# Loading the first four row tiles of x already cast, from GpSimd's queue

## The chip, the cores and the metric

The kernel runs on one core of one Trainium2 chip. A core has a matrix engine (TensorE, PE in the profile; PEld is its loading of weights), a vector engine (VectorE, DVE), an engine for activations and copies (ScalarE, ACT), GpSimd (POOL) and SyncE (SP), which here does nothing but issue transfers. Data move between the chip's memory and the core's on-chip memory (SBUF) by 16 DMA engines. The engines run on their own and wait for one another by semaphores; each works through its instructions in the order in which the program has them. The metric is the device time of one execution in microseconds (us), lower is better.

## What is computed

```python
def setup_inputs():
    B, S, D = 8, 2048, 2048
    # x: [B, S, D] float32, w: [D, D] float32, both normally distributed

def reference(x, w):
    cs = np.cumsum(x, axis=1)
    diff = cs - np.concatenate([zeros, cs[:, :-1, :]], axis=1)
    return np.matmul(diff, w).astype(np.float32)
```

The difference of a running sum is the sequence itself, so the output is x times w up to rounding: 16384 rows of x, in 128 row tiles of 128 rows, by a matrix of 2048 x 2048. The kernel computes that product and no running sum.

## The kernel before, in words

The 128 row tiles are worked in two ways. The first four (`PLAIN = 4`) are multiplied plainly in bf16, while w is still coming in. All others go in groups of four through a scheme of seven products for each two-by-two split, in f16, with scaled blocks of w that stay in SBUF; 31 such groups fill the time from about 70 us to the end. Which instruction comes when on each engine is written out by hand: every operation is recorded with a label (`record`), the table `places` gives each label a number for its period, and `emit` sorts by that number. So the numbers set only the order on each engine; the data dependences set the waits.

The opening stage is the one that the change touches (period 0 of `places`).

- w is loaded in 32 chunks of 512 KB (`fetch`, L281): label `w.h.ko` is rows 128 ko to 128 ko + 127, half h of the columns. Each chunk lands as f32 in its own place, `rest(h, ko)`. ScalarE then casts it to bf16 into a ring of seven buffers (`taken`, L287), and VectorE takes the largest magnitude of each row of it (L291), from which the scale of the f16 blocks comes (L402 to L409).
- x of the first four tiles is loaded in 16 pieces of 256 KB (`load_x`, L245): label `first x.q.r` is row tile r, columns 512 q to 512 q + 511. The pieces lie as f32 in places of w's second half that are not loaded yet (`resting(KH - 1 - q, a)`, which is the place of w.1.(7-q) or w.1.(15-q)). VectorE casts two row tiles at once to bf16 (`cast_x`, L251; label `cast x.q.a`, a = 0 for row tiles 0 and 1, a = 1 for 2 and 3) into `resting(q, 0)`, which is the place of w.1.q.
- TensorE transposes the eight 128 x 128 blocks of such a piece (`turn_x`, L260, label `turn x.q.a`) by an identity matrix, `eye`. VectorE (for q = 0) or ScalarE copies the result from PSUM into `xP` (`turned`, L270).
- The plain products are then `plain.h.r.ko` (L302): row tile r, chunk w.h.ko, two matmuls of 512 columns (one for row tile 3 with h = 0, whose other half is done late, `left over`, L430).
- The identity is made on VectorE: ones, a running count, its transpose, and four comparisons of 32 rows each (`eye_rows`, L220). In the order before, the first comparison stands early, and the other three behind the maximum of w.0.0.
- 22 matmuls on zeros (`warm.i`, L338) stand on TensorE before and between the first real ones.

All loads before the change, of x and of w, and all stores go out on SP's queue, in the order of `places`: first x.0.2, first x.0.3, w.0.0, first x.0.1, first x.0.0, w.0.3, and so on, the last piece of x (first x.3.2) between w.0.9 and w.0.11. GpSimd has nothing to do in this stage before the maximum over all partitions (L406). w.1.q can be loaded only when the transposes of x.q have read their place.

The order of TensorE in the opening: the first 15 warm matmuls, turn x.0.1, five warm ones, turn x.0.0, one warm, plain.0.2.0, one warm, plain.0.2.3, turn x.1.0, plain.0.2.1, plain.0.0.0, plain.0.0.3, plain.0.0.1, and on. Behind the plain stage follow the scaled blocks of w (L415, L417), the first tiles of the second kind (weighed at L138, scaled at L170, transposed by DMA at L187) and their products (L532, L554).

Of the kernel before, what the change touches and what calls it, by code (L numbers as in the profile page):

```python
# [10 lines left out]
def kernel(  # L11
# [6 lines left out]
    nc = tc.nc  # L18
    P = 128
# [39 lines left out]
        [p[:, i // 2, i % 2] for p in pieces] for i in range(8)  # L59
    )  # L60
    fours = Wall.bitcast(f16).rearrange("p k (i n j c) -> p k i j n c", i=4, j=2, c=NB)
    tiny = const.tile([P, 64], f32, name="tiny")
    sums_at = [tiny[:, ds(2 * i, 2)] for i in range(4)]
    means_at = [tiny[:, ds(i, 1)] for i in (8, 9, 13, 14)]
    uw, uinv, wred = (tiny[:, ds(10 + i, 1)] for i in range(3))
# [48 lines left out]
    def record(label, engine, ask):  # L114
        at = seen[period[0], label] = seen.get((period[0], label), 0) + 1
        if at > 1:
            label = f"{label}#{at}"
        ops.append((period[0], label, engine, ask))
# [90 lines left out]
    def resting(k, a):  # L209
        return whole[k][:, a, 1, :]  # L210
# [26 lines left out]
    for i in range(0, P, 32):  # L237
        eye_rows(i)

    def load_x(q, r):  # L240
        to = resting(KH - 1 - q, r // 2)[:, ds(r % 2 * NB, NB)]
        record(
            f"first x.{q}.{r}",
            "sp",
            lambda: nc.sync.dma_start(to, x2[ds(r * P, P), ds(q * KQ * P, KQ * P)]),  # L245
        )

    def cast_x(q, a):
        to = resting(q, 0).bitcast(bf16).rearrange("p (a c) -> p a c", a=2)[:, a]
        src = resting(KH - 1 - q, a)  # L250
        record(f"cast x.{q}.{a}", "dve", lambda: nc.vector.tensor_copy(to, src))  # L251
        return to

    def turn_x(q, a, src, i):
        v = banks[i].bitcast(bf16)
# [10 lines left out]
    def turned(q, a, v, engine):  # L266
        to = xP[:, ds(2 * a, 2), ds(q * KQ, KQ), :].rearrange("p r k m -> p r (k m)")
        v = v.rearrange("p (r c) -> p r c", r=2)
        on = nc.scalar.copy if engine == "act" else nc.vector.tensor_copy
        record(f"turned x.{q}.{a}", engine, lambda: on(to, v))  # L270
# [72 lines left out]
    AHEAD = 3  # L343
    done = []
    ps = [[banks[2 * r + n] for n in here(0, r)] for r in range(PLAIN)]
    loads = {2: 1, 5: 2, 9: 3}
    turns = {2: (1, 0), 3: (1, 1), 5: (2, 0), 6: (2, 1), 9: (3, 0), 10: (3, 1)}
    for ko in range(KO):
        for r in range(PLAIN):
            if ko in loads:  # L350
                load_x(loads[ko], r)
            elif ko < 2 and r // 2 == ko:
                load_x(0, r)
        fetch(0, ko)
    cast = {}
    for ko in range(KO - KQ):
        if ko == 0:
            for a in range(2):
                turned(0, a, turn_x(0, a, cast_x(0, a), 6 + a), "dve")
                if a == 0:  # L360
                    taken(0, ko)
                for r in (2 * a, 2 * a + 1):
                    plain(0, r, ko)
            continue
        if ko in turns:
            q, a = turns[ko]
            if a == 0:
                for i in range(2):
                    cast[q, i] = cast_x(q, i)
            v = turn_x(q, a, cast[q, a], 7)  # L370
            taken(0, ko)
            turned(q, a, v, "act")
        else:
            taken(0, ko)
        for r in range(PLAIN):
            plain(0, r, ko)
# [756 lines left out]
    for g in range(PLAIN + 4, END, 4):  # L1133
# [5 lines left out]

    places = {  # L1140
        0: {
            'ones': -4948, 'numbers': -4947, 'numbers turned': -4946, 'zeros': -4945,
# [524 lines left out]
```

## Time and profile before

| | us |
|---|---|
| median of 3 runs | 1461.22 |
| lowest and highest run | 1456.45, 1462.13 |
| span of the profiled execution | 1457.7 |
| TensorE busy | 1440.2 (99%) |
| VectorE busy | 1245.1 (85%) |
| ScalarE busy | 1132.1 (78%) |
| GpSimd busy | 288.1 (20%) |

The span reaches from the first to the last instruction of one execution that the hardware profiler recorded. That execution's own device time isn't listed beside it; the median of the runs lies 3.5 us above its span. The granted clock of TensorE was 0.999 over the span. A busy TensorE is not yet a TensorE at its peak, since matmuls are pipelined and their ends are modelled. In the lists of waits, a row names who waited, for whom, and for how many microseconds in total, how often, and at the longest. In the chain, a row is a piece of the path that ended last, with its start and length. Bandwidths are of the 16 DMA engines together.

### The profile page before, as it was taken

How to read it: one execution, taken by the hardware profiler on the slowest of the kernel's cores; microseconds unless marked ns; L12 is line 12 of the kernel's file. 1: busy time of each engine (PE TensorE's matmuls, PEld its weight loads, DVE VectorE, ACT ScalarE, POOL GpSimd, SP SyncE). 2: the span in 40 equal slices, each digit the busy share in tenths (PEclk: the TensorE clock that was granted, in tenths of full speed). 3: DMA queues.
4: the chain of work that ended last, by engine and by line, in shares of the span. 5: the costliest groups of instructions: out<-in, count | busy, mean ns of one | idle time of the engine just before them, and what ended most of it. 6: DMA issues, size and time to landing. Idle time of an engine off the chain costs nothing.

```text
span 1457.7 us, 20733 instructions
## 1 busy us (share of the span) xinstructions
PE 1440.2 (99%) x6692; PEld 652.4 (45%) x6698; DVE 1245.1 (85%) x2075; ACT 1132.1 (78%) x1742; POOL 288.1 (20%) x400
## 2 busy tenths in 40 slices
PE   8999999999999999999999999999999999999998
PEld 3444444444444444444444444444444444444443
DVE  6998898888888888889888889888888888898887
ACT  5886678877788877788877788877788777788773
POOL 0001122212222212222122122122122122122211
PEclk9999999999999999999999999999999999999999
DMA  9999879999888999889998889998899999889983
GB/s 354 359 255 274 220 222 250 261 263 249 252 242 241 262 266 243 239 248 243 273 269 238 236 249 240 272 258 248 223 263 247 266 253 260 224 247 260 263 212 135
DMA packets 348108, 367.33 MB, mean 252 GB/s; under 512 B 271456, under 2 KB 271456, under 8 KB 348000
## 3 DMA queue, kind: packets, MB, share of 16 engines
q1 hardware_dynamic: 348000, 366.02, 89.3%
q8 instruction: 52, 0.85, 0.2%
q14 instruction: 56, 0.46, 0.1%
HBM read 166.20 MB, written 134.74 MB: 206 GB/s over the span
## 4 chain that ended last, share of the span: by engine, by line
PE 92%; DMA 5%; ACT 1%; issue 1%; DVE 0%; SPq 0%; DVEq 0%; POOL 0%; ACTq 0%
PE b L554 60%; PE b L532 32%; DMA W<-in_w_dram 2%; DMA W<-in_x_dram 2%; DMA out_dram<-arena 0%; DMA x<-arena 0%; DMA F<-in_x_dram 0%; ACT waste L138 0%; ACT arena L287 0%; ACT F L170 0%; DVE arena L579 0%; ACT arena L318 0%; ACT arena L568 0%; ACT W L417 0%; SPq L245 0%
## 5 line engine op out<-in xcount | busy, mean ns | idle before, releaser
L532 PE MATMUL b<-W,x 128*128 128x512 f16 x2176 | 523.2, 379 | 0.6 <-DMA x<-F 0.6
L579 DVE SCALAR_TENSOR_TENSOR arena<-b,tiny,arena 128x512 f32<-128x512 f32 x612 | 439.7, 743 | 55.4 <-ACT arena L568 42.8
L554 PEld LDWEIGHTS <-arena 128*128 128x128 f16 x2700 | 264.0, 98 | 321.3 <-issue 3.5
L554 PE MATMUL b<-W,arena 128*128 128x512 f16 x1640 | 405.6, 379 | 0.6 <-ACT arena L571 0.6
L568 ACT ACTIVATE arena<-b,tiny 128x512 f32<-128x512 f32 x496 | 322.3, 685 | 51.4 <-PE b L532 39.4
L532 PEld LDWEIGHTS <-x 128*128 128x128 f16 x2176 | 212.9, 98 | 257.5 <-DMA x<-F 1.1
L170 ACT ACTIVATE F<-F,tiny 128x1024 f16<-128x1024 f32 x246 | 282.0, 1147 | 52.0 <-DVE tiny L159 47.0
L554 PE MATMUL b<-W,x 128*128 128x512 f16 x1180 | 297.1, 379 | 0.0
L571 ACT COPY arena<-b 128x512 f32<-128x512 f32 x294 | 169.7, 586 | 147.5 <-PE b L554 136.8
L138 ACT ACTIVATE waste<-F 128x1024 uint8<-128x1024 f32 x246 | 260.2, 1058 | 13.5 <-DMA F<-in_x_dram 11.7
L554 PE MATMUL b<-arena 128*128 128x512 f16 x1060 | 266.9, 379 | 0.5 <-DVE tiny L159 0.3
L520 POOL TENSOR_TENSOR arena<-x,x 128x512 f16<-128x512 f16 x118 | 142.7, 1210 | 543.9 <-PE b L554 511.9
L520 DVE TENSOR_TENSOR b<-b,arena 128x512 f32<-128x512 f32 x294 | 203.2, 692 | 38.1 <-ACT arena L571 37.3
L554 PEld LDWEIGHTS <-x 128*128 128x128 f16 x1416 | 138.5, 98 | 167.4 <-issue 0.7
L520 DVE TENSOR_TENSOR arena<-W 128x2048 f16<-128x2048 f16 (+1 forms) x127 | 149.4, 1177 | 2.8 <-PE b L554 2.5
L157 POOL TENSOR_SCALAR tiny<-tiny 128x1 f32<-128x1 f32 x124 | 41.8, 337 | 439.3 <-ACT waste L138 414.3
L571 ACT COPY b<-b 128x512 f32<-128x512 f32 x147 | 85.0, 578 | 35.8 <-DVE arena L579 20.6
L520 DVE TENSOR_TENSOR arena<-x,arena 128x512 f16<-128x512 f16 x118 | 50.2, 427 | 54.3 <-PE b L554 54.3
L520 DVE TENSOR_TENSOR x<-x,x 128x1024 f16<-128x1024 f16 x124 | 82.3, 681 | 0.2
L520 DVE TENSOR_TENSOR arena<-W,arena 128x2048 f16<-128x2048 f16 (+1 forms) x70 | 75.3, 1076 | 3.1 <-PE b L554 3.0
L160 POOL TENSOR_SCALAR tiny<-tiny 128x1 f32<-128x1 f32 x124 | 72.1, 583 | 0.7
L554 PE MATMUL b<-arena,x 128*128 128x512 f16 x236 | 60.2, 379 | 0.0
(46 smaller groups left out, 616.4 us busy)
## 6 DMA issues: line engine op xcount, KB each, us to landing
F<-in_x_dram SPq DMA_DIRECT2D x246, 512.0 KB, 5.5
out_dram<-arena SPq DMA_DIRECT2D x240, 512.0 KB, 5.4
W<-in_w_dram SPq DMA_DIRECT2D x32, 512.0 KB, 9.0
arena<-kept SPq DMA_DIRECT2D x29, 512.0 KB, 4.4
out_dram<-arena SPq DMA_DIRECT2D x32, 256.0 KB, 2.9
W<-in_x_dram SPq DMA_DIRECT2D x16, 256.0 KB, 7.6
x<-F SPq DMA_TRANSPOSE x246, 3.7
arena<-in_x_dram SPq DMA_DIRECT2D x2, 512.0 KB, 4.7
```

The costliest lines, as they stand in the source:

```text
L138: lambda: nc.scalar.activation(waste, data, ABS, scale=1.0 / ROW, accum_out=m),
L157: lambda: nc.gpsimd.tensor_scalar(m, m2[:, :1], m2[:, 1:], TINY, ADD, MAX),
L160: record(f"unit{role(t)}", "pool", lambda: nc.gpsimd.tensor_scalar(u, m, uw, None, MUL))
L170: lambda: nc.scalar.activation(to, data, COPY, scale=s),
L520: record(label, engine, lambda: on.tensor_tensor(dst, p, q, op))
L532: said = nc.tensor.matmul(to[n], a[k], b[k][:, n, :], start=(start and k == 0), stop=(k == KH - 1), skip_group_check=True,)
L554: said = nc.tensor.matmul(to, a[k], b[k], start=(start and k == 0), stop=(k == 3), skip_group_check=True)
L568: record(label, "act", lambda: nc.scalar.activation(c, p, COPY, scale=u))
L571: record(label, "act", lambda: nc.scalar.copy(to, p))
L579: label, "dve", lambda: nc.vector.scalar_tensor_tensor(c, p, u, c, MUL, ADD)
```

## The change

The sixteen f32 loads of x become eight transfers of two row tiles each, issued from GpSimd. They cast on the way, so that bf16 lands where the cast's result was put before, and the eight casts on VectorE are gone. Five of the eight stand behind a small copy on GpSimd ("seen") that reads one column of a chunk of w, and so waits until that chunk has landed; the copies' results go to a tile, `tiny`, that grows from 64 to 80 columns and are read by nobody. GpSimd's order is first x.0.1, first x.0.0, seen w.0.0, first x.1.0, first x.1.1, seen w.0.1, first x.2.0, seen w.0.6, first x.2.1, seen w.0.2, first x.3.0, seen w.0.7, first x.3.1. The four rows of the identity are made directly behind one another at the start of VectorE's order. The places of all other labels are kept.

```diff
-    tiny = const.tile([P, 64], f32, name="tiny")
+    tiny = const.tile([P, 80], f32, name="tiny")
...
-    def load_x(q, r):
-        to = resting(KH - 1 - q, r // 2)[:, ds(r % 2 * NB, NB)]
-        record(
-            f"first x.{q}.{r}",
-            "sp",
-            lambda: nc.sync.dma_start(to, x2[ds(r * P, P), ds(q * KQ * P, KQ * P)]),
-        )
-
-    def cast_x(q, a):
-        to = resting(q, 0).bitcast(bf16).rearrange("p (a c) -> p a c", a=2)[:, a]
-        src = resting(KH - 1 - q, a)
-        record(f"cast x.{q}.{a}", "dve", lambda: nc.vector.tensor_copy(to, src))
-        return to
+    def home_x(q, a):
+        return resting(q, 0).bitcast(bf16).rearrange("p (a c) -> p a c", a=2)[:, a]
+
+    def load_x(q, a, behind):
+        to = home_x(q, a).rearrange("p (r c) -> p r c", r=2)
+        src = x2[ds(2 * a * P, 2 * P), ds(q * KQ * P, KQ * P)].rearrange("(r p) c -> p r c", r=2)
+        if behind is not None:
+            seen_at = tiny[:, ds(64 + 4 * q + a, 1)]
+            first = rest(0, behind)[:, :1]
+            record(
+                f"seen.{q}.{a}", "pool", lambda: nc.gpsimd.tensor_copy(seen_at, first)
+            )
+        record(f"first x.{q}.{a}", "pool", lambda: nc.gpsimd.dma_start(to, src))
...
-    loads = {2: 1, 5: 2, 9: 3}
...
     for ko in range(KO):
-        for r in range(PLAIN):
-            if ko in loads:
-                load_x(loads[ko], r)
-            elif ko < 2 and r // 2 == ko:
-                load_x(0, r)
         fetch(0, ko)
-    cast = {}
+    for q, a, behind in (
+        (0, 1, None), (0, 0, None), (1, 0, 0), (1, 1, None), (2, 0, 1), (2, 1, 6), (3, 0, 2), (3, 1, 7)
+    ):
+        load_x(q, a, behind)
...
-                turned(0, a, turn_x(0, a, cast_x(0, a), 6 + a), "dve")
+                turned(0, a, turn_x(0, a, home_x(0, a), 6 + a), "dve")
...
-            if a == 0:
-                for i in range(2):
-                    cast[q, i] = cast_x(q, i)
-            v = turn_x(q, a, cast[q, a], 7)
+            v = turn_x(q, a, home_x(q, a), 7)
...
     places = {
         0: {
...
+            'first x.0.1': -4960, 'first x.0.0': -4959, 'seen.1.0': -4790, 'first x.1.0': -4789,
+            'first x.1.1': -4788, 'seen.2.0': -4600, 'first x.2.0': -4599, 'seen.2.1': -4598,
+            'first x.2.1': -4597, 'seen.3.0': -4440, 'first x.3.0': -4439, 'seen.3.1': -4400,
+            'first x.3.1': -4399, 'zeros': -4949, 'ones': -4948, 'numbers': -4947, 'numbers turned': -4946,
+            'eye': -4943, 'warm.0': -4870,
...
+            'max w.0.0': -4565, 'eye#2': -4942, 'w.0.4': -4511,
+            'eye#3': -4941, 'eye#4': -4940, 'turn x.0.1': -4470, 'warm.15': -4467, 'warm.16': -4465,
```

More of the change, by code (lines that the diff above doesn't have):

```diff
@@ L1141 @@
         0: {
-            'ones': -4948, 'numbers': -4947, 'numbers turned': -4946, 'zeros': -4945,
[10 rows of a table removed]
[3 rows of a table added]
+            'first x.3.1': -4399, 'zeros': -4949, 'ones': -4948, 'numbers': -4947, 'numbers turned': -4946,
[10 rows of a table added]
             'warm.19': -4410, 'w.0.7': -4406, 'turned x.0.1': -4390, 'turn x.0.0': -4354,
[2 rows of a table removed]
[2 rows of a table added]
             'max w.0.3': -4268, 'turned x.0.0': -4266, 'plain.0.2.3': -4263, 'turn x.1.0': -4243,
             'plain.0.2.1': -4220, 'turned x.1.0': -4215, 'plain.0.0.0': -4202, 'w.0.10': -4179,
[2 rows of a table removed]
[2 rows of a table added]
             'plain.0.3.0': -4075, 'turn x.1.1': -4072, 'plain.0.1.0': -4069, 'plain.0.1.3': -4068,
             'plain.0.1.6': -4067, 'plain.0.0.4': -4065, 'max w.0.1': -4049, 'turned x.1.1': -4028,
[2 rows of a table removed]
[2 rows of a table added]
             'plain.0.3.2': -3962, 'plain.0.1.1': -3957, 'cast w.0.7': -3940, 'plain.0.0.2': -3930,
```

37 rows, old and new, of the table places are left out of this document.

## The prediction

> **What bounds the kernel now.** I read the page's first part, then TensorE's waits over the whole span and again after 100 us, then the chain that ended last, then the first 60 us engine by engine. The first part of the page, and TensorE's waits (us in total, times, longest) over the whole span:
>
> ```profile
> PE 1440.2 (99%) x6692; PEld 652.4 (45%) x6698; DVE 1245.1 (85%) x2075; ACT 1132.1 (78%) x1742; POOL 288.1 (20%) x400
> ...
> PE b L260 <- DVE waste L220: 3.2, 1, 3.2
> PE b L532 <- DVE arena L520: 2.3, 1, 2.3
> PE b L302 <- ACT arena L287: 1.6, 2, 1.3
> PE b L532 <- DMA x<-F: 0.6, 1, 0.6
> PE b L430 <- DVE W L415: 0.5, 1, 0.5
> ```
>
> The same view from 100 us to the end:
>
> ```profile
> PE b L554 <- ACT arena L571: 0.6, 1, 0.6
> PE b L554 <- DVE tiny L159: 0.3, 1, 0.3
> PE b L554 <- DVE arena L579: 0.2, 1, 0.2
> ```
>
> After 100 us TensorE waits 0.6 + 0.3 + 0.2 = 1.1 us in 1358 us. So the end is set by how much of its work TensorE has done by about 95 us, and a microsecond lost or gained there goes through to the end. All that the change touches lies before 60 us. What holds that stage is in the chain (start, us, what):
>
> ```profile
> 2.59 6.90 DMA W<-in_x_dram
> 9.51 7.31 DMA W<-in_x_dram
> 16.83 8.41 DMA W<-in_x_dram
> 25.26 8.53 DMA W<-in_w_dram
> 33.80 10.22 DMA W<-in_w_dram
> 44.04 10.76 DMA W<-in_w_dram
> ...
> 59.67 1.04 ACT arena L287
> ...
> 78.44 5.58 DMA F<-in_x_dram
> 84.01 6.17 DMA x<-arena
> ```
>
> The chain is transfers, one behind the other, to 54.8 us; the last cast of w ends at 60.7, ScalarE's queue of work follows, and then the load and the transposes that TensorE's 2.3 us wait hangs on; they end at 90.2. By ten-microsecond stretches (busy us of PE, PEld, DVE, ACT, POOL with their counts, clock, DMA share, GB/s):
>
> ```profile
> 0.00:10.00 10.00, 4.83 (x15) 1.83 (x16) 3.90 (x10) 2.33 (x2) 0.19 (x4) 1.00 0.75 220
> 10.00:20.00 10.00, 8.53 (x61) 4.65 (x61) 6.29 (x9) 5.84 (x7) 0.00 (x0) 1.00 1.03 408
> 50.00:60.00 10.00, 9.95 (x47) 4.50 (x46) 9.79 (x10) 7.41 (x9) 0.00 (x0) 1.00 1.03 408
> ```
>
> From 10 us on the transfers are full at 408 GB/s; in the first ten they move 220. TensorE is nearly full too. So two clocks run side by side: the transfers pace the casts and maxima of w, and TensorE works off the plain products. The first sets when TensorE's waits behind the plain stage (those at L430 and L532: 0.5 + 0.6 + 2.3 = 3.4 us) end; the second has those 3.4 us of slack behind it.
>
> **The change, part by part.** TensorE's first stretches (start, us), and what fed them:
>
> ```profile
> 2.13 4.83 PE L338 MATMUL b<-arena 128*128 128x512 bf16 x15 [2.13 <-DVE arena L229]
> 10.15 0.61 PE L260 MATMUL b<-waste,W 128*128 128x128 bf16 x8 [3.19 <-DVE waste L220]
> 11.67 0.61 PE L260 MATMUL b<-waste,W 128*128 128x128 bf16 x8
> 12.33 0.59 PE L302 MATMUL b<-arena 128*128 128x512 bf16 x2
> 13.41 0.61 PE L260 MATMUL b<-waste,W 128*128 128x128 bf16 x8
> 15.29 2.67 PE L302 MATMUL b<-arena 128*128 128x512 bf16 x10 [1.27 <-ACT arena L287]
> 33.68 0.61 PE L260 MATMUL b<-waste,W 128*128 128x128 bf16 x8
> ...
> 5.80 0.70 DVE L251 CAST W<-W 128x1024 bf16<-128x1024 f32 x1 [3.66 <-DMA W<-in_x_dram]
> 7.99 1.22 DVE L291 TENSOR_REDUCE tiny<-W 128x1 f32<-128x1024 f32 x1 [1.50 <-DMA W<-in_w_dram]
> 9.23 0.87 DVE L220 TENSOR_SCALAR waste<-W 32x128 bf16<-32x128 f32 x3
> ...
> 14.19 1.04 ACT L287 CAST arena<-W 128x1024 bf16<-128x1024 f32 x1 [2.27 <-DMA W<-in_w_dram]
> 16.05 1.05 ACT L287 CAST arena<-W 128x1024 bf16<-128x1024 f32 x1
> 19.97 3.04 ACT L287 CAST arena<-W 128x1024 bf16<-128x1024 f32 x3
> ```
>
> *The identity first.* x.0.1 is cast by 6.5 us, yet its transposes start at 10.15, because three of the four eye rows stand behind the maximum of w.0.0 on VectorE. With all four ahead of it the 3.2 us wait goes. What is late next is the landing of x itself: in TensorE's order the first plain product stands behind turn x.0.0, and turn x.1.0 behind two products. So this part alone moves nothing until x.0.0 (now turned at 11.67) and x.1.0 (13.41) are there.
>
> *The casts off VectorE.* By groups of lines, in the first 60 us, the casts; then of the loads of w and of x the shortest, median and longest time to landing; then the tiny GpSimd operations of the whole page:
>
> ```profile
> L251 DVE CAST W<-W 128x1024 bf16<-128x1024 f32 x8 | 5.5, 692 | 9.1 <-DMA W<-in_x_dram 9.1
> ...
> DMA to landing us min/median/max: 6.3/9.0/10.8
> ...
> DMA to landing us min/median/max: 3.6/7.6/8.4
> ...
> L157 POOL TENSOR_SCALAR tiny<-tiny 128x1 f32<-128x1 f32 x124 | 41.8, 337 | 439.3 <-ACT waste L138 414.3
> ```
>
> 8 x 0.692 = 5.5 us of VectorE go, but VectorE stood 9.1 us waiting for x in front of them: they are bound by landings, not by VectorE. Per chunk of x, 0.7 us between landing and transposes is saved, if it lands as early. I count that as up to 0.7 us of TensorE's start and nothing later, since TensorE is full from 15.29 on.
>
> *Sixteen issues leave SP.* SP's queue is held by landings (medians 9.0 and 7.6 us), so w takes the freed places: w.0.0 goes out first, not third, and the same bytes follow. The total read is unchanged: 16 x 256 KB of x and 32 x 512 KB of w, 20.97 MB. Written into SBUF are 2.1 MB fewer.
>
> *Eight casting transfers of 512 KB (read) on POOL.* No row shows a transfer issued there, or one that casts. Their price is the unknown of the sum. From below: if a cast transfer occupies the DMA engines by what it writes, 2.1 MB / 408 GB/s = 5.1 us are gained. From above: if it runs at half the rate, 4.19 MB / 408 = 10.3 us are added; I see nothing that excludes either. I take the rate of the uncast transfer, as the nearest rows are loads of the same x in the same 2 KB runs: zero.
>
> *Five waits on POOL.* Five "seen" copies at 0.34 us are 1.7 us, on an engine that has nothing to do until 60 us. Each holds the transfers behind it until a chunk of w has landed: w.0.0, w.0.1, w.0.6, w.0.2, w.0.7, whose casts start at 7.99, 14.19, 16.05 and, the last two, among the three from 19.97 on, so by 21 us. So x.1.0 and x.1.1 are asked for at about 8 at the latest (w.0.0 goes out first now, so rather 6), x.2.0 at about 13, x.2.1 at 15, x.3.0 at 19 and x.3.1 at 21. With 7.6 us to landing x.3.1 is there at 29, before the 33.68 at which it is turned: hidden, and it costs TensorE about as much as it is later than that. The tight one is x.1.0: asked for at 6 to 8, landing at 12 to 15.5, where it is turned at 13.41 now.
>
> *The homes.* x now lands where its cast went, so w.1.0 to w.1.3 wait for the same transposes as before; w.1.4 to w.1.7 and w.1.12 to w.1.15 no longer wait for casts. SP was not held there; nothing. The tile "tiny" grows by 64 bytes, which moves what lies behind it; no row prices that, and I take zero.
>
> **The sum.** For the transfers' clock: the first 10 us move 220 x 10 = 2.2 MB where 408 would move 4.1, so the ramp costs (4.1 - 2.2)/408 = 4.6 us. Two queues with long 512 KB requests from the start should lift a part of it; a queue that starts later takes some back. I take -1 us (estimate; bounds 0 and -2.6, the ramp less the two microseconds that pass before the first transfer of the chain is under way). The cast rate: 0. TensorE's clock: first product some 1 to 2 us earlier, x.1.0 within 2 us of now either way, all of it inside the 3.4 us that it waits later for the transfers' clock. Sum: 1457.7 - 1 = 1456.7 us of span. The profiled execution gives a span only; the median of the runs, 1461.2, lies 3.5 above it, taken as launch and end. **1460 us**, own range 1456 to 1464.
>
> One row that bears on the start: VectorE is busy 3.90 us of the first ten, of which a cast (0.70), the maximum (1.22) and three eye rows (0.87) are known; 1.1 us are left for the memsets, the scan and the first eye row. The Trainium skill, "SBUF — State Buffer", section "SBUF: two separate sides", says that a transfer issued from GpSimd cannot have its descriptors written while VectorE runs an operation in a two-port mode, and names the fp32 copy within SBUF as one. By that rule the casts that go would have been the worst neighbours, and what is left could hold back the first two transfers by the 1.1 us and the eye rows' 0.87 at most; the sum by it would be 1461 to 1462. No run here shows it yet.
>
> **The rivals.**
> *Slow casts (slower).* Place: the DMA engines, 2 to 35 us. At half the rate the 4.19 MB of x cost 10.3 us more, the last chunk of w lands that much later, and the chain through the maximum, the scaled blocks and the loads behind them moves with it, since ScalarE's queue from 60.7 starts with the last cast. Time: 1461.2 + 10 = about 1471. It decides (7.3 us) from a cast rate of 0.58 of the uncast one down. For it: no row of such a transfer. Against it: nothing but the halved write.
> *Casts paid by the write (faster).* 5.1 us less transfer and a better ramp: TensorE must also start earlier, and can gain its later 3.4 us of waits, the 1.3 before 15.29 and about 2 from the start, 6.7 in all. Time: about 1455.
> *x starved (up to 3 us slower).* If x's queue gets a third of the bandwidth, as it would if 2 KB runs alternate with 4 KB runs: 220 to 290 GB/s give it some 90 at first, 524 KB take 5.5 us, and with 2 us to start x.0.0 is there at 13 and x.1.0, at the 408 then reached, at 17, where they are turned at 11.67 and 13.41 now. TensorE loses about 3.6 us, and between nothing and all of it reaches the end, as the 3.4 us of slack hold or not. Time: about 1463. The Trainium skill, "DMA: Bandwidth & Descriptors", section "Queues, rings and completion order", says that a DMA engine goes round its queues packet by packet; by it the shares hang on the packets, which no row here gives.
> *The change doesn't do what it says:* VectorE was not the bound at the casts, so if nothing but VectorE's work changes, the time is that of before, 1461; this is within my forecast's range.
>
> **How the numbers follow.** A measurement of this kernel tells about 0.5%, 7.3 us, from no change. Forecast, with no effect in it: 0.42, all within. Starved: 0.12, of which 0.02 beyond 7.3 us. Paid by the write: 0.15, of which 0.10 beyond. Slow casts: 0.31, nearly all beyond. Faster 0.10, slower 0.33, same 0.57. The range reaches from 1454 (most of the fast rival) to 1474 (the slow rival with some starving on top).
>
> **What would show it.** Right: the casts of w still paced by landings, 512 KB / 408 GB/s = 1.3 us apart where w has the queue alone; the last cast of w ends at 60 ± 1.5; the first transposes at 6 to 8.5 us, with x landing as their releaser; x.1.0 turned at 13 ± 2; GB/s at about 400 from 10 us on, counted by what is read. Wrong: the last cast of w at 65 or later (slow casts), or TensorE waiting for W<-in_x_dram again and again between 13 and 40 us (starved), or the chain leaving the transfers before 50 us (paid by the write). New waits of TensorE behind 100 us would point to the moved tiles.

## The result, and the profile after

The changed kernel takes 1462.34 us (median; its runs lie between 1460.6 and 1465.1), the kernel before 1460.14 us in the same comparison. The ratio is 1.0017, with a 95% interval of 1.0009 to 1.0024: by it the kernel is slower by 2.5 us, 1.3 to 3.5. That is inside the range and inside what was called no change, but it is on the other side of before than forecast. One run of each kernel was far slower (2142.2 us here, 3263.7 us of the kernel before, in a later comparison) and is left out of the ranges and ratios. The profiled execution has a span of 1463.2 us and a time of 1465.0, at the upper end of its runs, so its 5.5 us over the span of before are more than a typical run loses.

The first part of the page, and TensorE's waits over the whole span:

```profile
PE 1443.3 (99%) x6698; PEld 653.1 (45%) x6698; DVE 1241.8 (85%) x2067; ACT 1131.4 (77%) x1742; POOL 294.3 (20%) x413
...
PE b L260 <- DMA W<-in_x_dram: 8.3, 4, 5.3
PE b L526 <- DVE arena L514: 2.3, 1, 2.3
```

From 100 us to the end:

```profile
PE b L548 <- ACT b L565: 1.1, 2, 0.7
PE b L548 <- ACT arena L565: 0.5, 1, 0.5
PE b L548 <- DVE tiny L159: 0.3, 1, 0.3
PE b L548 <- DVE arena L573: 0.2, 1, 0.2
```

The wait for the identity is gone. In its place stand 8.3 us of waiting for x itself, in four pieces. The 2.3 us in front of the first product with S1g (one of the scheme's sums of blocks of x; L526, which was L532) are as they were. The first fifteen warm matmuls start 1 us earlier, because the label "zeros" moved ahead too, from -4945 to -4949, which the description of the change leaves out. TensorE's start (start, us), with what it waited for, and two later marks, the last of the eight transposes and the first product with S1g:

```profile
1.18 5.24 PE L338 MATMUL b<-arena 128*128 128x512 bf16 x15 [1.18 <-DVE arena L229]
11.73 1.03 PE L260 MATMUL b<-waste,W 128*128 128x128 bf16 x8 [5.31 <-DMA W<-in_x_dram]
12.56 2.34 PE L338 MATMUL b<-arena 128*128 128x512 bf16 x5
15.55 0.62 PE L260 MATMUL b<-waste,W 128*128 128x128 bf16 x8 [0.65 <-DMA W<-in_x_dram]
19.43 0.62 PE L260 MATMUL b<-waste,W 128*128 128x128 bf16 x8 [1.97 <-DMA W<-in_x_dram]
23.26 0.62 PE L260 MATMUL b<-waste,W 128*128 128x128 bf16 x8 [0.36 <-DMA W<-in_x_dram]
...
38.22 0.61 PE L260 MATMUL b<-waste,W 128*128 128x128 bf16 x8
...
93.91 5.17 PE L526 MATMUL b<-W,arena 128*128 128x512 f16 x16 [2.32 <-DVE arena L514]
```

Two of these marks before, turn x.1.1 and the first product with S1g:

```profile
17.79 0.61 PE L260 MATMUL b<-waste,W 128*128 128x128 bf16 x8
...
90.95 3.63 PE L532 MATMUL b<-W,arena 128*128 128x512 f16 x16 [2.27 <-DVE arena L520]
```

The first four transposes start at 11.7, 15.6, 19.4 and 23.3, one every 3.8 us, where before they started at 10.15, 11.67, 13.41 and 17.79. So TensorE is 5.5 us late at turn x.1.1, 4.5 at the last one (38.22 against 33.68), and 3.0 at the product with S1g (93.91 against 90.95). Of the 5.5 us by which this span is longer, those 3.0 are one part; the sixteen matmuls behind the wait take 1.5 us more, at a granted clock that fell to 0.50, and the waits behind 100 us are 1.0 us more (2.1 against 1.1). The landings themselves, in the sources' view of the eight transfers: how long the issue occupies GpSimd, and the shortest, median and longest time to landing:

```profile
L252 POOL DMA_DIRECT2D W<-in_x_dram x8: 713/713/1018, 1.3 to 17.4; - x8
...
DMA to landing us min/median/max: 10.4/17.2/19.4
```

A transfer is issued in 0.7 us and lands after 17 (median). The two queues between 12 and 30 us, when both always had work (packets, MB written, share of the 16 engines' time):

```profile
q1 hardware_dynamic: 1291, 4.70, 69.3%
q0 software_dynamic: 1288, 1.24, 40.7%
```

This is the row that says most of why. In 18 us SP's queue moved 1291 packets and GpSimd's 1288: one for one. But a packet of w is a run of 4 KB, and one of x a run of 2 KB that is read and of 1 KB that is written. So of what is read, x gets 2.48 MB of 7.18, 35%, or 138 GB/s, and 524 KB take 3.8 us. (Each transfer has 16 more small packets in these counts: 256 + 16 for x, 128 + 16 for w.)

The start is a second part. The first transfer of x is issued from 1.25 us on, yet between 4 and 6 us the queues moved

```profile
q1 hardware_dynamic: 159, 0.57, 87.0%
q0 software_dynamic: 2, 0.00, 0.6%
```

The first of these two packets of GpSimd's queue comes after 5.5 us. SP's queue, issued from 0.73 us on, moved its first packet before 2 us. One for one begins at about 8 us (140 against 141 from 8 to 10). So x.0.1 lands 10.4 us after its issue, and more than 4 of these pass before a packet of x moves; as the queue is never empty from there on, every later piece of x carries that delay too. Each kernel here that loads x from GpSimd shows it, with the first packet between 5.0 and 7.0 us. What fills that time was not tested.

The chain that ended last now runs through x and TensorE:

```profile
6.31 16.90 DMA W<-in_x_dram
23.26 0.62 PE b L260 x8
23.88 6.47 PE b L302 x30
...
38.86 0.33 SPq L281
...
39.29 5.95 DMA W<-in_w_dram
45.25 10.62 DMA W<-in_w_dram
```

It waits for x.1.1 to land, then for TensorE's work up to the last transposes, and only then for a transfer of w.

On the other side of the stage, ScalarE's waits for the transposes of x, its last two casts of w, and VectorE's final maximum, here and before:

```profile
ACT arena L270 <- PE b L260: 13.6, 5, 9.8
...
62.65 1.99 ACT L287 CAST arena<-W 128x1024 bf16<-128x1024 f32 x2 [0.78 <-PE b L302]
...
58.42 0.19 DVE L396 TENSOR_REDUCE tiny<-tiny 128x1 f32<-128x32 f32 x1
...
59.92 0.19 DVE L402 TENSOR_REDUCE tiny<-tiny 128x1 f32<-128x32 f32 x1
```

The final maximum over w is there at 58.4, 1.5 us earlier than before (59.92). The last cast ends at 64.6 instead of 60.7. ScalarE works in order; it waited 13.6 us in all to copy the transposes (L270; 1.3 before), with casts of w behind those copies, and the last wait ahead of the last casts is for TensorE to give a ring buffer back. Of the prediction's two clocks, that of the transfers gained, as forecast; TensorE's work was 5.5 us late at turn x.1.1, of which 3.0 were left at the product with S1g, and that is what shows at the end.

### The profile page after: what moved, and what is told of

It is laid out like the page before. It is cut to its first block, busy times and chain, and to the rows that moved or that the text cites. A ratio compares the mean times of both kernels' runs of the same rounds, so it can differ in the third digit from the quotient of the medians.

```text
span 1463.2 us, 20732 instructions
## 1 busy us (share of the span) xinstructions
PE 1443.3 (99%) x6698; PEld 653.1 (45%) x6698; DVE 1241.8 (85%) x2067; ACT 1131.4 (77%) x1742; POOL 294.3 (20%) x413
## 3 DMA queue, kind: packets, MB, share of 16 engines
q0 software_dynamic: 2176, 2.10, 0.8%
## 4 chain that ended last, share of the span: by engine, by line
PE 92%; DMA 5%; ACT 1%; issue 1%; DVE 1%; POOL 0%; SPq 0%; DVEq 0%; ACTq 0%; POOLq 0%
PE b L548 59%; PE b L526 32%; DMA W<-in_w_dram 1%; DMA out_dram<-arena 1%; DMA W<-in_x_dram 1%; PE b L302 1%; DMA x<-F 1%; DMA x<-arena 0%; DMA F<-in_x_dram 0%; DVE arena L514 0%; DVE arena L573 0%; ACT F L170 0%; ACT waste L138 0%; PE b L260 0%; ACT arena L562 0%
## 5 line engine op out<-in xcount | busy, mean ns | idle before, releaser
L526 PE MATMUL b<-W,x 128*128 128x512 f16 x2176 | 523.1, 379 | 0.0
L562 ACT ACTIVATE arena<-b,tiny 128x512 f32<-128x512 f32 x496 | 321.9, 685 | 53.9 <-PE b L526 38.9
L526 PEld LDWEIGHTS <-x 128*128 128x128 f16 x2176 | 212.9, 98 | 256.8 <-DMA x<-F 0.4
L138 ACT ACTIVATE waste<-F 128x1024 uint8<-128x1024 f32 x246 | 260.3, 1058 | 12.8 <-DMA F<-in_x_dram 10.7
## 6 DMA issues: line engine op xcount, KB each, us to landing
W<-in_w_dram SPq DMA_DIRECT2D x32, 512.0 KB, 10.2
W<-in_x_dram POOLq DMA_DIRECT2D x8, 256.0 KB, 17.2
```

Of the source, the lines that this page charges most:

```text
L138: lambda: nc.scalar.activation(waste, data, ABS, scale=1.0 / ROW, accum_out=m),
L526: said = nc.tensor.matmul(to[n], a[k], b[k][:, n, :], start=(start and k == 0), stop=(k == KH - 1), skip_group_check=True,)
L562: record(label, "act", lambda: nc.scalar.activation(c, p, COPY, scale=u))
```

## The experiments

The rival theories: **starved**, that x comes late because its small packets take turns with w's large ones, so that TensorE is late by more than its slack (the late first packet adds to this lateness, and no run sets it apart); **slow cast**, that casting on the way is what costs; and **clock**, that the loss is TensorE's halved clock behind its waits. All ratios are to the kernel before, with 95% intervals.

### The identity first, alone

```diff
-            'ones': -4948, 'numbers': -4947, 'numbers turned': -4946, 'zeros': -4945,
-            'first x.0.2': -4944, 'eye': -4909, 'first x.0.3': -4889, 'warm.0': -4870,
+            'ones': -4948, 'numbers': -4947, 'numbers turned': -4946, 'zeros': -4949,
+            'first x.0.2': -4944, 'eye': -4943, 'first x.0.3': -4889, 'warm.0': -4870,
...
-            'max w.0.0': -4565, 'eye#2': -4541, 'first x.2.1': -4533, 'w.0.4': -4511,
-            'eye#3': -4496, 'eye#4': -4490, 'turn x.0.1': -4470, 'warm.15': -4467, 'warm.16': -4465,
+            'max w.0.0': -4565, 'eye#2': -4942, 'first x.2.1': -4533, 'w.0.4': -4511,
+            'eye#3': -4941, 'eye#4': -4940, 'turn x.0.1': -4470, 'warm.15': -4467, 'warm.16': -4465,
```

> Before, with the identity made first and nothing else. If landings decide the start (starved), the first transposes come at about 6.6 to 7 us instead of 10.15, but TensorE still waits for the cast of w.0.1 until 15.3 and the end moves by less than 1 us: ratio 0.999 to 1.001 to the kernel before. If instead the identity's place was what cost the opening, the 3.2 us reach the end: about 0.998.

1460.37 us, ratio 1.0004 (0.9995 to 1.0013). The first transposes started at 7.00, and the wait moved on to the next things that were late:

```profile
PE b L260 <- DVE W L251: 2.7, 2, 2.2
PE b L302 <- ACT arena L287: 1.6, 1, 1.6
```

The casts that TensorE waits for (L251) had themselves waited 5.1 us for x to land. So this part of the change is worth nothing by itself that shows, as landings decide the start.

### The same transfers without the cast

```diff
-        to = home_x(q, a).rearrange("p (r c) -> p r c", r=2)
+        to = resting(KH - 1 - q, a).rearrange("p (r c) -> p r c", r=2)
...
+    def cast_x(q, a):
+        to, src = home_x(q, a), resting(KH - 1 - q, a)
+        record(f"cast x.{q}.{a}", "dve", lambda: nc.vector.tensor_copy(to, src))
+        return to
...
-            v = turn_x(q, a, home_x(q, a), 7)
+            v = turn_x(q, a, cast_x(q, a), 7)
...
```

> After, but the eight transfers from GpSimd do not cast: f32 lands in the old places and VectorE casts as before. If x is starved by the other queue, x.0.1 still lands later than 10 us, TensorE's waits for x before 25 us stay at 6 to 9 us and the ratio stays at 1.001 to 1.003. If the cast on the way is what is slow, x.0.1 lands by 7 us, the waits are under 3 us and the ratio falls to 1.000 or lower. The share of the engines' time of the software queue for the same 4.19 MB read tells the price of the cast: 20.7% of 60 us in after.

1458.88 us, ratio 0.9995 (0.9986 to 1.0003): the loss is gone. TensorE's waits for x, now behind VectorE's cast, are

```profile
PE b L265 <- DVE W L256: 6.2, 2, 5.8
```

The expectation of neither theory held as a whole: the waits stayed at 6.2 us, as starved says, and the time fell, as slow cast says. What happened is in the queues' rows, between 12 and 22 us of this kernel:

```profile
q0 software_dynamic: 548, 2.01, 52.2%
q1 hardware_dynamic: 545, 1.98, 50.7%
```

Again one for one, 548 packets against 545. But without the cast the two rows of 2 KB that follow each other in SBUF go as one packet of 4 KB (the eight transfers are 1152 packets in all, with the cast 2176), and so x gets half of the engines. It lands after 9.6 to 12.8 us instead of 10.4 to 19.4. Over the first 60 us its queue took 18.0% of the engines' time, against 20.7% in the changed kernel. So this run changed two things, the cast and the size of a packet, and could not tell them apart by its time.

### Wide rows: the cast stays, the packets grow

```diff
-        to = home_x(q, a).rearrange("p (r c) -> p r c", r=2)
-        src = x2[ds(2 * a * P, 2 * P), ds(q * KQ * P, KQ * P)].rearrange("(r p) c -> p r c", r=2)
+        to = home_x(q, a)
+        src = x2[ds(row_of[q, a] * P, P), ds(q // 2 * 2 * KQ * P, 2 * KQ * P)]
...
```

A piece is then one row tile and 1024 columns (`row_of` gives the tile); the copies out of PSUM go to that tile's place, and eight products of the opening stand later in TensorE's order.

> After, with each casting transfer taking one row tile and 1024 columns (runs of 4 KB read and 2 KB written) instead of two row tiles and 512 columns (runs of 2 KB and 1 KB); the bytes, the cast, the number of transfers and the waits are the same. If the two queues take turns by packets, x's part rises from a third to about a half: x.0.1 to landing 7 to 9 us instead of 10.4, median of the eight under 12 instead of 17.2, waits for x under 5 us, ratio 0.999 to 1.001. If the cast as such makes x late, whatever the runs: median 15 us or more, ratio 1.001 to 1.003.

The landing times came out as starved says. The eight transfers, and the two queues between 12 and 22 us:

```profile
L254 POOL DMA_DIRECT2D W<-in_x_dram x8: 527/528/859, 1.3 to 20.5; - x8
DMA to landing us min/median/max: 7.9/10.2/11.9
...
q0 software_dynamic: 558, 1.02, 53.9%
q1 hardware_dynamic: 560, 2.04, 53.9%
```

558 casting packets of 4 KB read against 560 of w, with the same share of the engines' time. So the cast itself costs next to nothing here: 53.9% of 16 engines over 10 us for 558 packets is 155 ns of an engine per packet, and for 560 packets of uncast w 154 ns. In the changed kernel, with packets of half the size, 40.7% over 18 us for 1288 is 91 ns, more than half of 155. In 1152 packets, as in the run without the cast, the eight transfers took 18.5% of the engines' first 60 us, against 18.0%. And what was read, 2.04 MB of each matrix in 10 us, is 408 GB/s, as in the kernel before without any cast. The median to landing falls from 17.2 to 10.2 us with the cast in place, which leaves nothing of the slow cast.

The time did not follow: 1462.12 us, ratio 1.0025 (1.0016 to 1.0034). TensorE's waits of this run say where it went:

```profile
PE b L262 <- DMA W<-in_x_dram: 3.8, 2, 3.4
PE b L303 <- ACT arena L271: 3.6, 4, 1.1
```

The waits for x fell from 8.3 to 3.8 us, but 3.6 us are new, for ScalarE's copy out of PSUM (L271), because in this layout the next product needs the tile that has just been transposed. The expectation of the ratio failed, since I had not counted that dependence.

### w in runs of 2 KB

```diff
-        record(
-            f"w.{h}.{ko}", "sp", lambda: nc.sync.dma_start(to, w[ds(ko * P, P), ds(h * NH, NH)])
-        )
+
+        def both():
+            for n in range(2):
+                said = nc.sync.dma_start(
+                    to[:, ds(n * NB, NB)], w[ds(ko * P, P), ds(h * NH + n * NB, NB)]
+                )
+            return said
+
+        record(f"w.{h}.{ko}", "sp", both)
```

> After, with each chunk of w loaded by two transfers of half the columns, so in runs of 2 KB as x's. If the queues take turns run by run, x's part of what is read goes from a third to about a half: x.0.1 to landing 7 to 8.5 us instead of 10.4, x transfers 2.6 us apart instead of 3.9, TensorE's waits for x about halved; ratio 0.999 to 1.001. If they share by transfers or by bytes, or if the cast is slow, x lands as late as in after and the ratio stays at 1.001 to 1.003.

x landed after 8.1 to 13.4 us (median 9.2), and TensorE's waits for it fell to 3.9 us. The time stayed: 1461.71 us, ratio 1.002 (1.0011 to 1.0028). From 10 to 20 us the queues moved 0.95 MB of x as written, so 1.90 as read, and 1.96 MB of w: x's share of what is read rose from 35% to 49%, as starved says. What x gained, w lost: 196 GB/s against 261 in the changed kernel between 12 and 30 us, and TensorE waited for casts of w instead (2.0 us). The engines together read 386 GB/s, against 399. So the time, which was expected at 0.999 to 1.001, is no evidence for starved, since the same edit slowed w.

### w held back for the first two transfers of x

```diff
+    record("hold", "sp", lambda: nc.sync.dma_start(tiny[:1, ds(79, 1)], resting(0, 0)[:1, :1]))
...
+            'hold': -4700,
```

> After, with one tiny transfer in SP's queue ahead of w.0.1 that reads x.0.0, so that of w only w.0.0 and w.0.3 share the engines with the first two transfers of x. Starved: x.0.1 lands at about 7 and x.0.0 at about 9 us instead of 11.7 and 15.5, TensorE's waits for x fall from 8.3 to under 4 us, and the time falls by 2 to 5 us against after, to a ratio of 0.997 to 1.000 to before. Slow cast: x.0.1 lands no more than 1 us earlier and the ratio stays at 1.001 or more.

1458.92 us, ratio 0.9995 (0.9987 to 1.0004). The cast, the packets, the software queue, the moved tile and the order of all else are as in the changed kernel; only w.0.1 and what follows stand behind the landing of x.0.0. The first transposes start at 8.81 and 10.34 instead of 11.73 and 15.55, and the waits become

```profile
PE b L302 <- ACT arena L287: 2.9, 1, 2.9
PE b L260 <- DMA W<-in_x_dram: 2.5, 2, 1.6
PE b L527 <- DVE arena L515: 2.1, 1, 2.1
```

8.3 us of waiting for x become 2.5, and the loss is gone; this interval and that of the changed kernel (1.0009 to 1.0024) do not overlap. w came later for it, the final maximum at 60.88 us against 58.42, and still the loss went; so it was x's lateness and not w's. It is the cleanest run for that. It also shows the late start of the queue: with only w.0.0 and w.0.3 beside it, the first packet of x still came after 5.0 us, and x.0.1 was turned at 8.81, where the kernel before had it cast by 6.5.

### Without the five waits on GpSimd

```diff
-        (0, 1, None), (0, 0, None), (1, 0, 0), (1, 1, None), (2, 0, 1), (2, 1, 6), (3, 0, 2), (3, 1, 7)
+        (0, 1, None), (0, 0, None), (1, 0, None), (1, 1, None), (2, 0, None), (2, 1, None), (3, 0, None), (3, 1, None)
```

> After, without the five copies on GpSimd that wait for chunks of w; all eight transfers of x are asked for at once. If x's queue is never empty in after because it gets a third of the engines, the waits cost nothing: x lands at the same spacing of 3.9 us, waits for x stay at 7 to 9 us, ratio 1.001 to 1.003. If the waits are what makes x late, x.1.0 is turned 2 us or more earlier than 19.4 and the ratio falls to 1.000.

1462.5 us, ratio 1.0025 (1.0015 to 1.0036). The first four transposes start at 11.85, 15.60, 19.48 and 23.31, as in the changed kernel within 0.1 us, and the waits for x are 7.9 us. x's queue was never empty, so what stands ahead of it on GpSimd costs nothing that shows.

### TensorE late by 3 us, and by 5.6 us, in the kernel before

```diff
+    for i in range(14):
+        record(
+            f"more.{i}",
+            "pe",
+            lambda: nc.tensor.matmul(
+                banks[7], xP[:, 2, 0, :], wb[0, 0][:, :NB], start=True, stop=True, skip_group_check=True
+            ),
+        )
...
+            'more.0': -4073, ...
```

The second kernel has `range(26)`.

> Before, with fourteen idle matmuls (3.0 us) on TensorE ahead of turn x.1.1, at about 18 us, so TensorE is late by 3 us in the plain stage and no transfer is. The prediction's slack: 3.4 us of later waits take them up, ratio 1.000. The ring: ScalarE's casts wait for TensorE to give the seven buffers back, so the last cast of w ends 2 to 3 us later (63 instead of 60.7), all that follows moves with it, TensorE's wait behind stays near 2 us, and the ratio is 1.0015 to 1.0025.

> Before, with 26 idle matmuls (5.6 us) on TensorE ahead of turn x.1.1, which makes TensorE as late as it is in after at that place (23.3 instead of 17.8 us) while all transfers stay as they are. If TensorE's lateness is the whole loss of after, the slack takes about 3 of the 5.6 us and the ratio is 1.0015 to 1.0025, with the last cast of w ending 2 to 4 us later than 60.7. If after loses by something else (transfers, software queue), TensorE's lateness alone leaves 1.000 to 1.001.

With 14 more: 1459.82 us, ratio 1.0007 (0.9997 to 1.0016). With 26: 1463.89 us, ratio 1.0036 (1.0023 to 1.0048). The last casts of w, of the kernel with 14 and then of that with 26:

```profile
59.64 1.99 ACT L287 CAST arena<-W 128x1024 bf16<-128x1024 f32 x2 [0.78 <-PE b L302]
```

```profile
65.50 1.99 ACT L287 CAST arena<-W 128x1024 bf16<-128x1024 f32 x2 [0.78 <-PE b L302]
```

They end at 61.6 and 67.5 us. Neither pair of expectations held: with 14 the ratio lies between the two that were named and its interval takes in no change, and the last cast ends 0.9 us late, not 2 to 3; with 26 more is lost than the 1.0015 to 1.0025 expected, and the last cast ends 6.8 us late, not 2 to 4.

The transfers of x were left as before, so TensorE's lateness alone is enough for a loss, and the loss grows with it. How late TensorE is at two places against the kernel before, in one profiled execution each, and the loss by the ratio with its interval, all in us:

| | turn x.1.1 | first product with S1g | loss |
|---|---|---|---|
| 14 more | 2.5 | 0.2 | 1.0 (-0.4 to 2.3) |
| the changed kernel | 5.5 | 3.0 | 2.5 (1.3 to 3.5) |
| 26 more | 8.3 | 4.7 | 5.3 (3.4 to 7.0) |

Between the two places 2.3 to 3.6 us are taken up; what is left is about what the medians lose. The execution with 26 had also opened at half the clock (0.66 from 10 to 20 us) and was the slowest of its five runs, so its 8.3 is more than a typical run of it has.

### The clock

Ten matmuls, whose result is overwritten, ahead of the first product with S1g, in the changed kernel and in the kernel before; and in the kernel before with the identity first also ten more warm ones, two ahead of turn x.1.0 and seven ahead of plain.0.2.1.

```diff
+        for i in range(10):
+            record(
+                f"busy.{i}",
+                "pe",
+                lambda: nc.tensor.matmul(
+                    V[0], A12h[0], B21[0][:, 0, :], start=True, stop=True, skip_group_check=True
+                ),
+            )
         product("S1g T1", V, S1g, T1, True)
```

> After, with ten matmuls whose result is overwritten, ahead of the first matmul that waits for S1g (TensorE's 2.3 us wait at 91.6). If the halved clock behind that wait is part of the loss, the sixteen matmuls behind it take 3.5 us instead of 5.0, the mean clock rises from 0.997 to 0.998 or 0.999 and the time falls by about 1.5 us against after: ratio 1.000 to 1.001. If the clock has nothing to do with the wait, no change: 1.0015 to 1.002.

> Before, with the same ten matmuls. Its runs lie between 1457 and 1462 us; if that spread is the same clock, falling or not behind the same wait, the upper runs go and the median falls by 1 to 2 us, ratio 0.9985 to 0.9995. If the spread has another source: 1.000.

> Before, with the identity first, with matmuls whose results are overwritten in TensorE's waits of the first 16 us (ten more warm ones, two ahead of turn x.1.0, seven ahead of plain.0.2.1) and the ten of the run above. If in the run with the identity alone the gain at the start was lost to a halved clock between 15 and 20 us, this keeps the clock up there (10 matmuls from 15.3 in 2.7 us instead of 4.0) and the ratio falls to 0.997 to 0.999. If the identity's place is worth nothing in itself: as the run before with the ten alone.

In the changed kernel: 1463.27 us, ratio 1.0032 (1.0021 to 1.0043). Behind the wait the clock did what was expected (the mean over the runs stayed at 0.997), and the time did not:

```profile
92.49 2.32 PE L794 MATMUL b<-W,x 128*128 128x512 f16 x10
94.65 3.62 PE L526 MATMUL b<-W,arena 128*128 128x512 f16 x16
```

The sixteen matmuls behind the wait take 3.6 us instead of 5.2, but the median is not lower: neither expectation (1.000 to 1.001, or 1.0015 to 1.002) held. The ten matmuls ran on to the start of the product, at 94.65, 0.7 us later than in the changed kernel, so they may have used up what the clock gained. In the kernel before: 1459.03 us, ratio 0.9999 (0.9991 to 1.0008), and its runs spread from 1457.2 to 1461.7 as without it. With the opening filled as well: 1459.22 us, ratio 1.0002 (0.9992 to 1.0012), though TensorE worked from 14.74 on at the full clock and the product with S1g came at 89.60. The clock explains part of what the one profiled execution lost, and not the difference of the medians. What speaks most against it are the runs without the cast: their mean granted clock was 0.997, as low as that of the changed kernel's runs (0.997; 0.998 of the kernel before), and they lost nothing. The clock also doesn't explain the spread of the kernel before.

### Wide rows and the hold together

```diff
+        to = home_x(q, a)
+        src = x2[ds(row_of[q, a] * P, P), ds(q // 2 * 2 * KQ * P, 2 * KQ * P)]
...
+    record("hold", "sp", lambda: nc.sync.dma_start(tiny[:1, ds(79, 1)], resting(0, 0)[:1, :1]))
...
+            'hold': -4700,
```

> The wide rows and the tiny transfer that holds w.0.1 back until x.0.0 has landed, together. If the lateness of x is the whole loss, this is no slower than before: ratio 0.998 to 1.000. If something else in after costs 2 us (the software queue as such, the moved tile), it stays at 1.001 or more.

1463.4 us, ratio 1.0034 (1.0021 to 1.0046). x came early (median 7.9 us to landing), but TensorE waited 3.5 us for ScalarE's copies, as with the wide rows alone, and 3.6 us for the first cast behind the hold. By the expectation's words something else than x's lateness would cost 2 us. The waits point at this kernel's own layout and at the hold; that these are all of it was not tested.

All profiled executions together bear out TensorE's lateness as the loss. The first product with S1g starts at 89.0 to 91.5 us in the kernel before and in the six with a ratio of 0.9995 to 1.0007, and at 92.6 to 95.7 us in the seven with 1.0017 to 1.0036. Starting it earlier than before (89.0 and 89.6, the two kernels with the identity first) gained nothing that shows. No kernel here is measurably faster than the one before; the two best, at 0.9995, are level with it.

## Why the prediction was wrong

**The bound** was read rightly in part: behind 100 us TensorE waits 1.1 + 0.5 + 0.3 + 0.2 = 2.1 us in the profiled execution against 1.1, so most of the loss is made ahead of that, and the end follows TensorE's work by about 95 us. That the transfers of w would go on setting the opening, with TensorE's work in slack behind them, failed: the chain now goes from x.1.1's landing through TensorE.

**The transfers' clock** was forecast 1 us faster and the final maximum came 1.5 us earlier. The price of the cast, the unknown of the sum, was taken as that of the uncast transfer, and this is what the packets show: 155 ns against 154 for the same run read. At the run that this kernel reads, 2 KB, a packet took 91 ns, more than half. Both rivals on it, the slow cast and the cast paid by the write, fall.

**The step that failed** is the landing of x. I took the time from issue to landing from before, 7.6 us, and put x.1.0 at 12 to 15.5 us (6 + 7.6 would be 13.6, not 12) and x.3.1 at 29; the median was 17.2 us, and x.1.0 was turned at 19.4. It was not asked for too late: the five transfers behind a wait were issued at 5.6 to 17.4 us, earlier than forecast. Time to landing was no property of the transfer. Before, x stood in one queue with w, in the order written, and its 7.6 us were mostly the queue ahead of it (256 KB at 408 GB/s are 0.6 us). Beside a second queue that is always full, it is the packets that share, and x's were the small ones; and the new queue took over 4 us from its first issue to its first packet. The forecast had x.1.0 within 2 us of 13.41 either way; it was 6.0 us late.

**The rival x starved** had the mechanism: a third of the bandwidth if 2 KB runs alternate with 4 KB runs, 1463 us (1462.3). Its sign came too: TensorE waited for x again at 15.55, 19.43 and 23.26. Its times for x.0.0 and x.1.0, 13 and 17, were about 2.5 us early (turned at 15.6 and 19.4), and it gave the queue 2 us to start, where more than 4 passed. It got a chance of 0.12 because no row of before gives the shares. The rule of the Trainium skill that was cited beside it ("DMA: Bandwidth & Descriptors", "Queues, rings and completion order": the engines go round the queues packet by packet) agrees with the traces, 1288 to 1291, 548 to 545 and 558 to 560; how many packets an engine takes from one queue before it turns to the other, these counts don't show. Weighed as a mechanism, it was the one statement at hand on two full queues, and should have had the larger chance.

**The slack of 3.4 us** came near in size by luck. 2.5 us were taken up between turn x.1.1 and the product with S1g, and only in part by the waits that it was added up from: those of 0.5 and 0.6 (and one of 0.4 at L302) are gone, but the largest, the 2.3 us ahead of S1g, is there in both kernels (2.27 and 2.32). What it waits for moves with TensorE, since ScalarE's casts wait for transposes and ring buffers, and the chain for the last of w starts at the last transposes.

**The step from the span to the time**, 3.5 us "taken as launch and end", had no such source: nearly every run here takes 1.7 to 1.9 us more than its span. The rest was the spread between single runs.

**The identity first** did what was said, the 3.2 us wait went and the next late thing took its place; alone it is worth nothing (1.0004). **The waits on GpSimd** were hidden, as said, though for another reason: the queue they feed was never empty. **The homes and the moved tile** cost nothing that shows: with x in time the changed kernel is level with before. SP was held after all (12.7 us until x had landed and 4.1 us until it was transposed), but from 32 to 36 us the engines still read 395 GB/s. **The rule on VectorE's two-port mode** (the Trainium skill, "SBUF — State Buffer", "SBUF: two separate sides"), weighed at up to 2 us, is neither shown nor ruled out. The first issue took 1.02 us and the others 0.71. But the first packet of x came after 5.5 us, more than 2 us behind the last operation for the identity on VectorE (3.36), and no run tells what held it.

## What to carry to other kernels

When a load moves to a second queue, don't carry over its time to landing: write down for both queues the size of a packet, and give each the bandwidth in that proportion as long as the other is full (here 35% of what was read at 2 KB against 4 KB, and half at equal size). Look also for the time that the new queue takes to its first packet, here over 4 us. A cast on the way is then cheap if its runs are as long as the neighbour's, and the loads that the first work needs are better placed ahead in one full queue, or the other queue is held until they are there; here that brought the time back to that of before and not below it.

## What the runs showed that I had not expected

- A cast from f32 to bf16 on the way took no more of a DMA engine than a plain load of the same run read: 155 ns for 4 KB read with it, 154 without; 91 ns for 2 KB.
- Two rows of 2 KB that follow each other in SBUF went as one packet when they were copied, and as two when they were cast: 1152 packets against 2176 for the same eight shapes.
- The granted clock is 0.50 from 94 to 96 us, behind a wait of 2.32 us (the changed kernel); 0.66 over 10 to 20 us, behind one of 3.22 us (the kernel with 26 more matmuls); it is 0.69 over 90 to 95 us, behind one of 2.14 us (w held back); it stays at 1.00 behind waits of 2.27 and 3.19 us (the kernel before). The length alone doesn't decide it here.
- Single runs of the kernel before spread from 1455.2 to 1462.7 us. With TensorE's waits filled, 11 and 12 runs spread over 4.5 and 4.1 us, 31 of the kernel before beside them over 6.8, which doesn't decide it; the 11 runs without the cast spread over 1.7 us. The source stays open.
